# Third instead of fourth: the order of products in seven-product blocks, and three sums that change hands

## The chip, the cores and the metric

The kernel runs on one core of a Trainium2 chip. The metric is device time in microseconds (us) of one execution; a version's time is the median of several executions. The profile is one profiled execution, which traces every instruction with its start, its duration and what it waited for.

## The reference

A two-layer decoder trunk on 256 tokens of width 1024, in float32. Each layer is an FFN, an attention, and a second FFN, each behind an RMS norm and with a residual. The first layer's attention is stick-breaking; the second's is a sliding window with sinks that reads a K/V computed from the stream between the layers. So there are four FFNs, in the order FFN 1, attention, FFN 2, FFN 3, attention, FFN 4:

```python
D_MODEL, SEQ, DEPTH, D_FF = 1024, 256, 2, 2816

def swiglu(x, w_in, w_out):
    gate, up = jnp.split(x @ w_in, 2, axis=-1)
    return (jax.nn.silu(gate) * up) @ w_out

for layer in range(DEPTH):
    h = h + 0.5 * swiglu(rms_norm(h, ffn1_norm[layer]), ffn1_w_in[layer], ffn1_w_out[layer])
    ...                                   # attention, h = h + o @ w_o
    h = h + 0.5 * swiglu(rms_norm(h, ffn2_norm[layer]), ffn2_w_in[layer], ffn2_w_out[layer])
return rms_norm(h, final_norm)
```

## The kernel before

**A product.** A float32 product is made from three matmuls of the type fp32r: each operand is split in a high and a low half, and high x high, low x high and high x low are added up. ScalarE makes the high half of a weight tile (a cast, `w_hi`, L418), VectorE the low half by subtraction (`w_lo`, L420), in two pieces of 128x1024 for each megabyte of weights. A product (`product`, L619) takes a 512x512 piece of weights from its split (L405) through four steps of three matmuls, twelve 512-column matmuls, into one PSUM bank. All matmuls are issued at L287.

**The FFN.** The 2816 columns of an FFN are worked off in blocks: FFN 1 has a plain block, a narrow one of 256 columns and four seven-product blocks of 512 columns; FFNs 2 to 4 have one narrow block (block 0) and five seven-product blocks (blocks 1 to 5). Nineteen seven-product blocks in all, made by `strassen` (L773). The input is cut in 2 x 2 quarters: token half 0 or 1, and upper or lower half of the 1024 features. The weights of a block are cut in 2 x 2 as well: r11 and r21 are the gate's columns on the upper and lower features, r12 and r22 those of the up branch. r21 is thus the lower left piece. Instead of eight quarter products, seven are made, with S0 to S3, sums of the input's quarters that are made once in each FFN (`operand_sums`), and with sums of the weights. Before the change they stand in this order; a, d and b are the block's three PSUM banks:

| | weights | input | into bank | weights' sum made ahead |
|---|---|---|---|---|
| P1 | r11 | token half 0, upper | a | - |
| P2 | r11 | S0 | d | r11 += r12 (sum 0) |
| P3 | r22 | S3 | d, added | - |
| P4 | r21 | token half 0, lower | b | - (the plain product on the lower left weights) |
| P5 | r11 | S1 | a, added | r11 += r22 (sum 1) |
| P6 | r12 | S2 | a, added | r12 += r22 (sum 2) |
| P7 | r11 | token half 1, lower | a, added | r11 += r21 (sum 3) |

Between them stand copies by ScalarE that must be done before the next product adds into the same bank: bank a into b after P1 (L797, in most blocks), bank d into the tile `p5` after P2 (the profile's `p`, L781), bank a into `u2` after P5 (the profile's `u`, L781). VectorE adds banks to them (L785) and multiplies (L788); TensorE turns the result round (`turn`, L676).

**Sums.** A sum is made in one of two ways. `add` (L605) lets VectorE add two pieces of 128x1024 (L610); the right side is then the loaded tile. `fetch` (L614) issues from GpSimd's queue a transfer that reads the megabyte of weights from HBM once more and adds it to the tile in SBUF as it lands (L615), after whoever used the tile's old value has done so. Before the change every seven-product block makes sums 0 and 1 by VectorE and sums 2 and 3 by an adding transfer: 38 such transfers in the FFNs, and three more in the first attention. GpSimd's queue holds, beside these, the small powers of the norms (L522).

**Buffers.** Weights are loaded over SP's queue (`load`, L379) into six tiles of a megabyte, which are handed out in the order in which they were put back: a block takes four, the output weights of the block before take two in turn.

**The output product.** The FFN's second matmul (`out`, L866, `out_step`, L862) on the result of block n - 1 is listed in block n between P6 and P7: eight steps behind the narrow block 0, sixteen behind a seven-product block, a step being three matmuls.

**The order on the engines.** No queue's order is written by hand. The code lists tasks with engine, estimated duration and dependencies (`Plan`); a list scheduler (`listed`, `order`, L195) then simulates all queues. TensorE takes the listed order but, where the next step isn't ready in the simulation, the next one that is; all others take the task with the earliest due time, and the due times come from TensorE's order in the pass before, in up to four passes. The result is a fixed sequence of instructions for each engine with semaphores between. On the chip each engine works its sequence off strictly in order.

Of the kernel before, what the change touches and what calls it, by code (L numbers as in the profile page):

```python
# [18 lines left out]
D = 1024  # L19
# [20 lines left out]
PIECES = 2  # L40
ADDING = 170.0
PLAIN = 330.0
BY_DMA = False
DMA3 = True
FSUMS = 5000.0
TM = 1000.0
BOOST = 10000.0
# [11 lines left out]
LATE = (True, True, True)  # L59
KVFIRST = True  # L60
KVLATE = 3000.0
C11_0 = False
BL_LATE = 0.0

# [149 lines left out]
def dve(n):  # L214
    return n / 0.96 + 70
# [11 lines left out]
def kernel(  # L227
# [34 lines left out]
    RAW, WP, A4 = Slots("raw", RAWS, 8), Slots("w", HL, 8), Slots("a", 4, 4)  # L262
# [17 lines left out]
    def ts(t):  # L280
        return slice(t * P, (t + 1) * P)
# [7 lines left out]
    def B(*bs):  # L289
        return [(b, 0) for b in bs]  # L290
# [109 lines left out]
    def flat(buf):  # L400
        return buf.ap.rearrange("p a b -> p (a b)")
# [3 lines left out]
    def split(raw, prio=None):  # L405
        prio = plan.pos - LEAD if prio is None else prio
        a, b = raw.ab
        if raw.cut == 4:
            return split_fine(raw, prio)
        hi, lo = WP.get([P, a, b], F32R, "w_hi"), WP.get([P, a, b], F32R, "w_lo")  # L410
        m = a * b // PIECES
        for j in range(PIECES):
            sl = slice(j * m, (j + 1) * m)
            ks = [j] if PIECES == 2 else [0, 1]
            rs = [2 * j, 2 * j + 1] if raw.cut == 4 else ks

            first = [(xh, (0, 0))] if raw.cut == 4 and j == 1 else []
            T("ACT", act(m), lambda sl=sl: ACT.copy(out=flat(hi)[:, sl], in_=flat(raw)[:, sl]),  # L418
              r=[(raw, i) for i in rs] + first, w=[(hi, i) for i in ks], prio=prio)
            T("DVE", dve(m), lambda sl=sl: DVE.tensor_sub(out=flat(lo)[:, sl], in0=flat(raw)[:, sl],  # L420
                                                          in1=flat(hi)[:, sl].bitcast(F32)),
              r=[(raw, i) for i in rs] + [(hi, i) for i in ks], w=[(lo, i) for i in ks], prio=prio)
        return hi, lo
# [22 lines left out]
    def by_k(w):  # L446
        return w.rearrange("(k p) n -> p k n", p=P)
# [23 lines left out]
    def of_x(t, k):  # L471
        return ((lambda: xh.ap[:, k, ts(t)], lambda: xl.ap[:, k, ts(t)]), [(xh, (t, k // 4)), (xl, (t, k // 4))])
# [129 lines left out]
    def of_sums(SH, SL, i):  # L602
        return lambda kk: ((lambda: SH.ap[:, i, kk], lambda: SL.ap[:, i, kk]), [(SH, i), (SL, i)])

    def add(dst, src):  # L605
        m = 2048 // PIECES
        for i in range(PIECES):
            sl = slice(m * i, m * i + m)
            ks = [i] if PIECES == 2 else [0, 1]
            T("DVE", dve(m), lambda sl=sl: DVE.tensor_add(out=flat(dst)[:, sl], in0=flat(dst)[:, sl], in1=flat(src)[:, sl]),  # L610
              r=[(src, k) for k in ks], w=[(dst, k) for k in ks], prio=plan.pos - LEAD)


    def fetch(dst, src):  # L614
        T("POOL", 1500, lambda: nc.gpsimd.dma_start(out=dst.ap, in_=src, accum_op=ALU.add), w=[(dst, 0), (dst, 1)],  # L615
          prio=plan.pos - LOADS, lat=500.0)
        T("SP", P * 2048 * 4 / ADDING, lambda: None, w=[(dst, 0), (dst, 1)], prio=plan.pos - LOADS)

    def product(bank, raw, xs, first, last, at=0.0):  # L619
        w = split(raw)  # L620
        for kk in range(4):
            step(bank, w, kk, xs(kk), first and kk == 0, last and kk == 3)
        WP.put(*w)

    def ffn(w_in, w_out, acc, rest, finish, kv=None, blocks=BLOCKS, roots=None, ending=False, there=False, arranged=False):

        first, late = arranged, roots is not None
        wi, wo = by_k(w_in), by_k(w_out)  # L630
        wi4 = w_in.rearrange("(j p k) n -> p j k n", j=2, k=4)
        ring = [banks[i] for i in rest[0:3]]
# [16 lines left out]
        def of_s(i):  # L649
            return of_sums(SH, SL, i)  # L650

        def col(h, i, c, n=512):
            cs = slice(h * DFF + c, h * DFF + c + n)
            return wi4[:, i, :, cs] if first else wi[:, 4 * i:4 * i + 4, cs]

        def silu(dst, src, r, w, t, n=512):
            if late:
                T("ACT", act(n, True), lambda: ACT.activation(out=dst(), in_=src(), func=AF.Silu, scale=roots[t][0].ap), r=r + B(roots[t][0]) + [(consts, "tbl")], w=w)
            else:
                T("ACT", act(n), lambda: ACT.activation(out=dst(), in_=src(), func=AF.Silu), r=r + [(consts, "tbl")], w=w)  # L660
# [9 lines left out]
        def turn(m, t, aT, nk=4):  # L670
            n = nk * P
            view = lambda b: (lambda: b.ap[:, 0:nk, ts(t)])

            def run():
                for i in range(nk):
                    PE.transpose(out=tr.ap[:, i * P:(i + 1) * P], in_=m.ap[:, i * P:(i + 1) * P], identity=ident)  # L676
            T("PE", 109 * nk, run, r=B(m) + ID, w=B(tr))
            STG.put(m)
            part_to(tr, (aT[0], t, view(aT[0])), (aT[1], t, view(aT[1])), n,
                    lambda: tr.ap[:, 0:n].rearrange("p (a b) -> p a b", a=nk))  # L680
# [92 lines left out]
        def strassen(n, c, between):  # L773
            a, d, b = ring
            ring[:] = [d, b, a]
            aT = new_a()
            r11, r12, r22, r21 = [load([(slice(0, 512), col(h, i, c))], 4, 512) for h, i in ((0, 0), (1, 0), (1, 1), (0, 1))]

            def stage(src, name):
                s = STG.get([P, 512], F32, name)  # L780
                T("ACT", act(512), lambda: ACT.copy(out=s.ap, in_=src.ap), r=B(src), w=B(s), prio=plan.pos - STAGE)  # L781
                return s

            def plus(s, bank):
                T("DVE", dve(512), lambda: DVE.tensor_add(out=s.ap, in0=s.ap, in1=bank.ap), r=B(bank), w=B(s))  # L785

            def mul_less(dst, a_, b_, r, w, t):
                T("DVE", dve(512), lambda: DVE.scalar_tensor_tensor(out=dst(), in0=b_(), scalar=roots[t][1].ap if late else -1.0, in1=a_(),  # L788
                                                                    op0=ALU.mult, op1=ALU.mult),
                  r=r + (B(roots[t][1]) if late else []), w=w, lat=LAT["DVE"] + TM)  # L790

            product(a, r11, lambda kk: of_x(0, kk), True, False)
            c11 = C11 and (n != 1 or blocks[0] == "p" or C11_0)
            if c11:
                T("ACT", act(512), lambda: ACT.copy(out=b.ap, in_=a.ap), r=B(a), w=B(b), prio=plan.pos - STAGE)  # L797
                s1 = STG.get([P, 512], F32, "s1")
            else:
                s1 = stage(a, "s1")  # L800
            add(r11, r12)
            product(d, r11, of_s(0), True, False)
            p5 = stage(d, "p5")
            if BY_DMA:
                fetch(r11, col(1, 1, c))
            else:
                add(r11, r22)
            if DMA3:
                fetch(r12, col(1, 1, c))
            else:  # L810
                add(r12, r22)
            product(d, r22, of_s(3), False, True)
            RAW.put(r22)
            product(b, r21, lambda kk: of_x(0, 4 + kk), not c11, True)
            RAW.put(r21)
            if c11:
                silu(lambda: s1.ap, lambda: b.ap, B(b), B(s1), 0)
            else:
                plus(s1, b)
                silu(lambda: s1.ap, lambda: s1.ap, [], B(s1), 0)  # L820
            product(a, r11, of_s(1), False, False)
            fetch(r11, col(0, 1, c))
            u2 = stage(a, "u2")
            plus(u2, d)
            mul_less(lambda: s1.ap, lambda: s1.ap, lambda: u2.ap, B(u2), B(s1), 0)
            STG.put(u2)
            turn(s1, 0, aT)
            product(a, r12, of_s(2), False, False)
            RAW.put(r12)
            plus(p5, a)  # L830
            between()
            product(a, r11, lambda kk: of_x(1, 4 + kk), False, True)
            RAW.put(r11)
            m = STG.get([P, 512], F32, "m")
            silu(lambda: m.ap, lambda: a.ap, B(a), B(m), 1)
            mul_less(lambda: m.ap, lambda: m.ap, lambda: p5.ap, B(p5), B(m), 1)
            STG.put(p5)
            turn(m, 1, aT)
            return aT, 4
# [300 lines left out]
    def shared_kv(vec, other):  # L1140
# [25 lines left out]
        def run(ring, tr):  # L1166
# [19 lines left out]
            at_ = plan.pos  # L1186
            plan.pos += KVLATE
            for t in range(NT):
# [404 lines left out]
```

## Time and profile before

| | |
|---|---|
| median of 3 executions | 911.58 us (910.59 to 912.58) |
| profiled execution: its own time | 910.39 us |
| profiled execution: its span, first to last instruction | 908.6 us |
| mean granted TensorE clock | 0.998 |
| seven-product blocks of FFN 2, FFN 3, FFN 4, about | 307 to 455, 492 to 640, 739 to 892 us |

PE is TensorE, DVE is VectorE, ACT is ScalarE, POOL is GpSimd, SP the queue that issues plain loads. In a row of the timeline the columns are start, duration, engine, line, operation, output <- inputs and shapes; in brackets stands the engine's idle time ahead of it and what ended it. Matmuls overlap and their ends are modelled: a 512-column matmul is shown as 0.39 us long, but the next one starts about 0.23 us after it. Pauses shorter than the overlap are seen in the distance between starts only. In a row of windows each engine has its busy time and, in brackets, its instructions. Names of tiles stand without their numbers: `w_lo,S_h` is a matmul of the low half of weights with the high half of an input sum, `xT` the plain input, `aT` the operand of the output product.

### The profile page before, as it was taken

How to read it: one execution, taken by the hardware profiler on the slowest of the kernel's cores; microseconds unless marked ns; L12 is line 12 of the kernel's file. 1: busy time of each engine (PE TensorE's matmuls, PEld its weight loads, DVE VectorE, ACT ScalarE, POOL GpSimd, SP SyncE). 2: the span in 40 equal slices, each digit the busy share in tenths (PEclk: the TensorE clock that was granted, in tenths of full speed). 3: DMA queues.
4: the chain of work that ended last, by engine and by line, in shares of the span. 5: the costliest groups of instructions: out<-in, count | busy, mean ns of one | idle time of the engine just before them, and what ended most of it. 6: DMA issues, size and time to landing. Idle time of an engine off the chain costs nothing.

```text
span 908.6 us, 11840 instructions
## 1 busy us (share of the span) xinstructions
PE 897.5 (99%) x4420; PEld 739.5 (81%) x4420; DVE 818.3 (90%) x989; ACT 650.1 (72%) x935; POOL 66.7 (7%) x71
## 2 busy tenths in 40 slices
PE   9999999999999999999999999999999999999997
PEld 6888888888888888888888878888897787788886
DVE  8989989687977999998889999999788799999985
ACT  7867667786986876776688767667857677677662
POOL 2001000000000101010000101010000001101000
PEclk9999999999999999999999999999999999999999
DMA  9997999995763499999795999998944149999951
GB/s 337 349 238 223 289 298 233 285 291 154 239 206 115 104 267 306 246 290 268 211 343 127 255 264 266 284 318 225 335 129 163 47 107 287 284 250 291 323 148 47
DMA packets 107305, 214.43 MB, mean 236 GB/s; under 512 B 6256, under 2 KB 27760, under 8 KB 107248
## 3 DMA queue, kind: packets, MB, share of 16 engines
q1 hardware_dynamic: 85184, 170.49, 52.6%
q0 software_dynamic: 21648, 42.99, 26.9%
q8 instruction: 34, 0.56, 0.2%
q10 hardware_dynamic: 416, 0.20, 0.1%
q14 instruction: 23, 0.19, 0.1%
HBM read 212.62 MB, written 1.05 MB: 235 GB/s over the span
## 4 chain that ended last, share of the span: by engine, by line
PE 89%; DVE 8%; ACT 2%; issue 1%; DMA 0%; DVEq 0%; ACTq 0%
PE ps L287 85%; DVE w_lo L420 4%; PE ps L676 2%; ACT w_hi L418 1%; PE ps L490 1%; DVE raw L610 1%; DVE e L1319 0%; PE ps L1327 0%; DMA hN<-in_x_dram 0%; DVE s L586 0%; DVE small L1293 0%; DVE S_l L580 0%; ACT u L781 0%; DVE aT_l L497 0%; DVE o_l L1359 0%
## 5 line engine op out<-in xcount | busy, mean ns | idle before, releaser
L420 DVE TENSOR_TENSOR w_lo<-raw,w_hi 128x1024 fp32r<-128x1024 f32 x424 | 499.8, 1219 | 24.7 <-ACT w_hi L418 23.1
L418 ACT CAST w_hi<-raw 128x1024 fp32r<-128x1024 f32 x424 | 423.0, 1049 | 102.9 <-DVE raw L610 40.0
L287 PE MATMUL ps<-w_hi,xT 128*128 128x512 f32 (+1 forms) x788 | 229.8, 375 | 0.0
L287 PEld LDWEIGHTS ps<-w_hi,xT 128*128 128x128 f32 x788 | 142.7, 188 | 26.6 <-DVE xT L497 0.5
L287 PE MATMUL ps<-w_lo,xT 128*128 128x512 f32 (+1 forms) x394 | 146.8, 373 | 0.0
L287 PE MATMUL ps<-w_hi,aT_h 128*128 128x512 f32 x354 | 139.9, 395 | 0.0
L287 PE MATMUL ps<-w_lo,aT_h 128*128 128x512 f32 x354 | 137.7, 389 | 0.0
L287 PE MATMUL ps<-w_hi,aT_l 128*128 128x512 f32 x354 | 137.5, 388 | 0.0
L287 PE MATMUL ps<-w_hi,S_h 128*128 128x512 f32 x320 | 127.3, 398 | 2.0 <-ACT u L781 1.2
L287 PE MATMUL ps<-w_lo,S_h 128*128 128x512 f32 x320 | 124.9, 390 | 0.0
L287 PE MATMUL ps<-w_hi,S_l 128*128 128x512 f32 x320 | 124.8, 390 | 0.0
L610 DVE TENSOR_TENSOR raw<-raw 128x1024 f32<-128x1024 f32 x78 | 94.6, 1220 | 0.5
L615 POOL DMA_DIRECT2D raw<-in_ffn_w_in_dram x38 | 48.3, 1271 | 507.2 <-DVE w_lo L420 255.3
L287 PEld LDWEIGHTS ps<-w_lo,xT 128*128 128x128 f32 x394 | 74.2, 188 | 13.6 <-DVE w_lo L420 0.4
L287 PEld LDWEIGHTS ps<-w_lo,aT_h 128*128 128x128 f32 x354 | 66.4, 188 | 13.9
L287 PEld LDWEIGHTS ps<-w_hi,aT_l 128*128 128x128 f32 x354 | 66.6, 188 | 13.0
L287 PEld LDWEIGHTS ps<-w_hi,aT_h 128*128 128x128 f32 x354 | 66.5, 188 | 12.8
L287 PEld LDWEIGHTS ps<-w_hi,S_h 128*128 128x128 f32 x320 | 60.1, 188 | 16.8 <-ACT u L781 3.2
L287 PEld LDWEIGHTS ps<-w_lo,S_h 128*128 128x128 f32 x320 | 60.1, 188 | 13.0 <-DVE w_lo L420 0.2
L287 PEld LDWEIGHTS ps<-w_hi,S_l 128*128 128x128 f32 x320 | 60.2, 188 | 11.5
L496 ACT CAST aT_h<-ps 128x512 fp32r<-128x512 f32 (+1 forms) x48 | 26.3, 549 | 49.4 <-PE ps L676 49.2
L287 PE MATMUL ps<-xT,w_hi 128*128 128x512 f32 (+1 forms) x136 | 47.0, 394 | 0.0
(184 smaller groups left out, 941.7 us busy)
## 6 DMA issues: line engine op xcount, KB each, us to landing
raw<-in_ffn_w_in_dram SPq DMA_DIRECT2D x76, 1024.0 KB, 7.5
raw<-in_ffn_w_out_dram SPq DMA_DIRECT2D x44, 1024.0 KB, 8.2
raw<-in_ffn_w_in_dram POOLq DMA_DIRECT2D x38, 1024.0 KB, 10.0
raw<-in_sb_w_qkv_dram SPq DMA_DIRECT2D x12, 1024.0 KB, 8.0
raw<-in_ffn_w_in_dram SPq DMA_DIRECT2D x16, 512.0 KB, 6.4
raw<-in_ffn_w_in_dram SPq DMA_DIRECT2D x16, 256.0 KB, 5.4
raw<-in_sb_w_o_dram SPq DMA_DIRECT2D x4, 1024.0 KB, 5.3
raw<-in_swa_w_q_dram SPq DMA_DIRECT2D x4, 1024.0 KB, 9.0
```

The source lines that it names most:

```text
L287: PE.matmul(ps, lhsT=lhsT, rhs=rhs, start=start, stop=stop, skip_group_check=True)
L418: T("ACT", act(m), lambda sl=sl: ACT.copy(out=flat(hi)[:, sl], in_=flat(raw)[:, sl]), r=[(raw, i) for i in rs] + first, w=[(hi, i) for i i ...
L420: T("DVE", dve(m), lambda sl=sl: DVE.tensor_sub(out=flat(lo)[:, sl], in0=flat(raw)[:, sl], in1=flat(hi)[:, sl].bitcast(F32)), r=[(raw, i) ...
L490: PE.matmul(bank.ap[:, i * P:(i + 1) * P], lhsT=s, rhs=ident, start=i == 0, stop=True, is_transpose=True, skip_group_check=True)
L496: T("ACT", act(n), lambda: ACT.copy(out=hi[2](), in_=src()), r=B(bank), w=[hi[0:2]])
L610: T("DVE", dve(m), lambda sl=sl: DVE.tensor_add(out=flat(dst)[:, sl], in0=flat(dst)[:, sl], in1=flat(src)[:, sl]), r=[(src, k) for k in ks ...
L615: T("POOL", 1500, lambda: nc.gpsimd.dma_start(out=dst.ap, in_=src, accum_op=ALU.add), w=[(dst, 0), (dst, 1)], prio=plan.pos - LOADS, lat=5 ...
L676: PE.transpose(out=tr.ap[:, i * P:(i + 1) * P], in_=m.ap[:, i * P:(i + 1) * P], identity=ident)
```

## The change

A table `SPECIAL` now tells for each seven-product block, by the number of the FFN and of the block, who makes the four sums (V for VectorE, D for an adding transfer), in which order P3 and P4 are listed ((2, 3): P4 first), and behind which product the output product of the block before is listed (4 is the old place, and all have it).

In 18 of the 19 blocks P4 is listed ahead of P3; the 14 of FFNs 1 to 3 (four, five and five; the entry for FFN 1's narrow block is unused) keep their sums as they were. In FFN 4, block 1 keeps the old order of P3 and P4 and makes three sums by adding transfers (sum 1 too); blocks 3 and 4 make sum 3 by VectorE instead of a transfer; blocks 2 and 5 keep theirs. Adding transfers in the FFNs: 38 + 1 - 2 = 37. Additions by VectorE at L610: 78 - 2 + 4 = 80 pieces. r21's tile is put back after its split, which now is ahead of r22's, or, where VectorE makes sum 3, after that sum. `fill` and `stage_` only carry the place and the count.

```diff
--- before.py
+++ after.py
@@ -40,8 +40,6 @@
 PIECES = 2
 ADDING = 170.0
 PLAIN = 330.0
-BY_DMA = False
-DMA3 = True
 FSUMS = 5000.0
 TM = 1000.0
 BOOST = 10000.0
@@ -59,6 +57,7 @@
 LATE = (True, True, True)
 KVFIRST = True
 KVLATE = 3000.0
+SPECIAL = {(1, 1): ('VVDD', (2, 3), 4), ... (4, 1): ('VDDD', (3, 2), 4), (4, 2): ('VVDD', (2, 3), 4), (4, 3): ('VVDV', (2, 3), 4), (4, 4): ('VVDV', (2, 3), 4), (4, 5): ('VVDD', (2, 3), 4)}
 C11_0 = False
 BL_LATE = 0.0
 
@@ -624,9 +623,12 @@
 
 
 
+    stage_ = []
+
     def ffn(w_in, w_out, acc, rest, finish, kv=None, blocks=BLOCKS, roots=None, ending=False, there=False, arranged=False):
 
         first, late = arranged, roots is not None
+        stage_.append(0)
         wi, wo = by_k(w_in), by_k(w_out)
         wi4 = w_in.rearrange("(j p k) n -> p j k n", j=2, k=4)
         ring = [banks[i] for i in rest[0:3]]
@@ -798,37 +800,52 @@
                 s1 = STG.get([P, 512], F32, "s1")
             else:
                 s1 = stage(a, "s1")
-            add(r11, r12)
+            makers, second, filled = SPECIAL.get((len(stage_), n), ("VVDD", (3, 2), 4))
+
+            def fill(q):
+                if q == filled:
+                    between()
+
+
+            def summed(i, dst, src, h, k):
+                if makers[i] == "D":
+                    fetch(dst, col(h, k, c))
+                else:
+                    add(dst, src)
+
+            summed(0, r11, r12, 1, 0)
             product(d, r11, of_s(0), True, False)
             p5 = stage(d, "p5")
-            if BY_DMA:
-                fetch(r11, col(1, 1, c))
-            else:
-                add(r11, r22)
-            if DMA3:
-                fetch(r12, col(1, 1, c))
-            else:
-                add(r12, r22)
-            product(d, r22, of_s(3), False, True)
-            RAW.put(r22)
-            product(b, r21, lambda kk: of_x(0, 4 + kk), not c11, True)
-            RAW.put(r21)
+            summed(1, r11, r22, 1, 1)
+            summed(2, r12, r22, 1, 1)
+            for q in second:
+                if q == 3:
+                    product(d, r22, of_s(3), False, True)
+                    RAW.put(r22)
+                else:
+                    product(b, r21, lambda kk: of_x(0, 4 + kk), not c11, True)
+                    if makers[3] == "D":
+                        RAW.put(r21)
             if c11:
                 silu(lambda: s1.ap, lambda: b.ap, B(b), B(s1), 0)
             else:
                 plus(s1, b)
                 silu(lambda: s1.ap, lambda: s1.ap, [], B(s1), 0)
+            fill(6)
             product(a, r11, of_s(1), False, False)
-            fetch(r11, col(0, 1, c))
+            summed(3, r11, r21, 0, 1)
+            if makers[3] != "D":
+                RAW.put(r21)
             u2 = stage(a, "u2")
             plus(u2, d)
             mul_less(lambda: s1.ap, lambda: s1.ap, lambda: u2.ap, B(u2), B(s1), 0)
             STG.put(u2)
             turn(s1, 0, aT)
+            fill(7)
             product(a, r12, of_s(2), False, False)
             RAW.put(r12)
             plus(p5, a)
-            between()
+            fill(4)
             product(a, r11, lambda kk: of_x(1, 4 + kk), False, True)
             RAW.put(r11)
             m = STG.get([P, 512], F32, "m")
```

More of the change, by code (lines that the diff above doesn't have):

```diff
@@ L61 @@
 KVLATE = 3000.0
+SPECIAL = {(1, 1): ('VVDD', (2, 3), 4), (1, 2): ('VVDD', (2, 3), 4), (1, 3): ('VVDD', (2, 3), 4), (1, 4): ('VVDD', (2, 3), 4), (1, 5): ('VVDD', (2, 3), 4), (2, 1): ('VVDD', (2, 3), 4), (2, 2): ('VVDD', (2, 3), 4), (2, 3): ('VVDD', (2, 3), 4), (2, 4): ('VVDD', (2, 3), 4), (2, 5): ('VVDD', (2, 3), 4), (3, 1): ('VVDD', (2, 3), 4), (3, 2): ('VVDD', (2, 3), 4), (3, 3): ('VVDD', (2, 3), 4), (3, 4): ('VVDD', (2, 3), 4), (3, 5): ('VVDD', (2, 3), 4), (4, 1): ('VDDD', (3, 2), 4), (4, 2): ('VVDD', (2, 3), 4), (4, 3): ('VVDV', (2, 3), 4), (4, 4): ('VVDV', (2, 3), 4), (4, 5): ('VVDD', (2, 3), 4)}
 C11_0 = False
```

## The prediction

> **What bounds the kernel now.** I read the page first: shares, chain, groups, queues.
>
> ```profile
> span 908.6 us, 11840 instructions
> ...
> PE 897.5 (99%) x4420; PEld 739.5 (81%) x4420; DVE 818.3 (90%) x989; ACT 650.1 (72%) x935; POOL 66.7 (7%) x71
> ...
> q1 hardware_dynamic: 85184, 170.49, 52.6%
> q0 software_dynamic: 21648, 42.99, 26.9%
> ...
> PE 89%; DVE 8%; ACT 2%; issue 1%; DMA 0%; DVEq 0%; ACTq 0%
> ...
> L610 DVE TENSOR_TENSOR raw<-raw 128x1024 f32<-128x1024 f32 x78 | 94.6, 1220 | 0.5
> L615 POOL DMA_DIRECT2D raw<-in_ffn_w_in_dram x38 | 48.3, 1271 | 507.2 <-DVE w_lo L420 255.3
> ...
> raw<-in_ffn_w_in_dram POOLq DMA_DIRECT2D x38, 1024.0 KB, 10.0
> ```
>
> TensorE bounds it: 89% of the chain, and neither order nor sums change how many matmuls there are. So the change can only win or lose pauses of TensorE. Next come the windows, one for the blocks of each of the FFNs 2 and 3, and the last FFN cut in three.
>
> ```profile
> core 0: us, PE busy (x) PEld busy (x) DVE busy (x) ACT busy (x) POOL busy (x), PEclk, DMA share, GB/s
> 307.00:455.00 148.00, 148.00 (x671) 121.98 (x670) 142.05 (x144) 103.73 (x125) 11.53 (x9) 1.00 0.88 254
> 492.00:640.00 148.00, 147.44 (x666) 120.87 (x665) 143.06 (x143) 104.80 (x126) 11.49 (x9) 1.00 0.91 259
> 739.00:816.00 77.00, 75.53 (x337) 60.87 (x337) 76.59 (x80) 55.40 (x68) 6.39 (x5) 1.00 0.91 253
> 816.00:860.00 44.00, 44.00 (x202) 36.36 (x201) 41.90 (x41) 29.04 (x33) 3.84 (x3) 1.00 0.99 311
> 860.00:892.00 32.00, 32.00 (x148) 26.52 (x147) 27.50 (x28) 20.03 (x25) 1.28 (x1) 1.00 0.53 126
> ```
>
> The first half of the last FFN stands out: VectorE works 76.59 of 77.00 us there and TensorE has gaps of 1.47; afterwards TensorE has none and VectorE has 2.1 + 4.5 us to spare. VectorE makes the low halves of the weights, so in that half TensorE lives from hand to mouth. "PE busy" hides small pauses, because matmuls overlap; the spacing of their starts shows them. The chain gives the undisturbed pace:
>
> ```profile
> 786.35 15.70 PE ps L287 x69
> ```
>
> 15.70 / 69 = 0.2275 us. In the timeline of TensorE these are the largest pauses among the blocks that the change touches (last FFN, blocks 2, 2 and 3; FFN 3, blocks 4 and 2):
>
> ```profile
> 769.91 0.39 PE L287 MATMUL ps<-w_lo,S_h 128*128 128x512 f32 x1
> 770.97 0.50 PE L287 MATMUL ps<-w_hi,S_h 128*128 128x512 f32 x1 [0.68 <-ACT p L781]
> 771.31 0.39 PE L287 MATMUL ps<-w_hi,S_l 128*128 128x512 f32 x1
> ...
> 781.15 0.39 PE L287 MATMUL ps<-w_lo,S_h 128*128 128x512 f32 x1
> 782.21 0.50 PE L287 MATMUL ps<-w_hi,S_h 128*128 128x512 f32 x1 [0.68 <-ACT u L781]
> 782.55 0.39 PE L287 MATMUL ps<-w_hi,S_l 128*128 128x512 f32 x1
> ...
> 813.00 0.39 PE L287 MATMUL ps<-w_lo,aT_h 128*128 128x512 f32 x1
> 813.51 0.50 PE L287 MATMUL ps<-w_hi,S_h 128*128 128x512 f32 x1
> 813.84 0.39 PE L287 MATMUL ps<-w_hi,S_l 128*128 128x512 f32 x1
> ...
> 587.83 0.39 PE L287 MATMUL ps<-w_lo,xT 128*128 128x512 f32 x1
> 588.24 0.50 PE L287 MATMUL ps<-w_hi,S_h 128*128 128x512 f32 x1
> 588.58 0.40 PE L287 MATMUL ps<-w_hi,S_l 128*128 128x512 f32 x1
> ...
> 533.41 0.39 PE L287 MATMUL ps<-w_lo,aT_h 128*128 128x512 f32 x1
> 534.33 0.50 PE L287 MATMUL ps<-w_hi,S_h 128*128 128x512 f32 x1 [0.54 <-ACT u L781]
> 534.67 0.40 PE L287 MATMUL ps<-w_hi,S_l 128*128 128x512 f32 x1
> ```
>
> Each costs its wait and a slow second start. 769.91 to 771.31 is 1.40 for two steps of 0.2275: 0.94 us lost. Likewise 781.15 to 782.55: 0.94; 813.00 to 813.84: 0.84 - 0.455 = 0.39; 587.83 to 588.58: 0.75 - 0.455 = 0.29; 533.41 to 534.67: 0.81. Together 3.37 us, nearly all that there is to win. The last one waits for the copy u, which the change does not move, in an FFN whose sums stay as they are: I leave it.
>
> **The change, part by part.** *The order.* P4 now stands between P2 and P3. It adds no instruction. At 770.97 TensorE had ended P2 and could not start P3, which adds into the same bank, until ScalarE had copied that bank (p). P4 writes another bank and fits in. In most blocks it already does in part: the planner draws two of P4's four steps forward (at 588.24 they stand ahead of the wait), and there a full P4 instead of half changes nothing but the 0.29 at 588. P4's own bank must be free:
>
> ```profile
> 768.97 0.69 ACT L658 ACTIVATE m<-ps,small 128x512 f32<-128x512 f32 x1 [2.14 <-PE ps L287]
> 769.70 0.57 ACT L797 COPY ps<-ps 128x512 f32<-128x512 f32 x1
> 770.33 0.59 ACT L781 COPY p<-ps 128x512 f32<-128x512 f32 x1
> ```
>
> The copy into it ends at 770.27, P2 at 769.91 + 0.23 = 770.14: P4 starts about 0.2 late. Credit 0.94 - 0.2 = 0.74 here, and 0.29 at 588. In turn r21's split is due 2.72 us (12 x 0.2275) earlier and r22's 2.72 later; these are the same VectorE pieces in another order, and r21's buffer instead of r22's comes free first for the next block's r11: priced at nothing, because the next block's loads wait for whichever comes first. On SP's queue the loads of r21 and r22 may swap, which moves either by one transfer, 2.9 us of the DMA engines (52.6% of 908.6 / 163 transfers, the 170.49 MB of q1); half of P4 stood in third place before, so r21 was wanted there already. Past 816 VectorE's 6.6 us of idle time cover it; where they are gone, a swapped split costs one piece, 1.2 us.
>
> *Block 1 of the last FFN.* The sum r11 + r22 leaves VectorE (two pieces):
>
> ```profile
> 737.49 1.22 DVE L420 TENSOR_TENSOR w_lo<-raw,w_hi 128x1024 fp32r<-128x1024 f32 x1
> ...
> 744.56 1.22 DVE L610 TENSOR_TENSOR raw<-raw 128x1024 f32<-128x1024 f32 x1
> 745.70 1.22 DVE L420 TENSOR_TENSOR w_lo<-raw,w_hi 128x1024 fp32r<-128x1024 f32 x1
> ```
>
> Starts lie 1.14 apart (744.56 to 745.70), so VectorE is 2.28 us earlier from block 1's second half on. TensorE's pauses are what VectorE needed to keep up, so relief here is what lets pauses go: 0.94 at 782 (P6 waits for the copy u, and any ready step of the FFN's output product would fill it), and about half of the 0.39 at 813, say 0.2 (there the copy also queued behind a cast). The relief is spent by that: 0.74 + 0.94 + 0.2 = 1.88 of 2.28.
>
> In exchange comes a second adding transfer, of r22 into r11, between P2's split and P5's.
>
> ```profile
> 735.37 1.32 POOL L615 DMA_DIRECT2D raw<-in_ffn_w_in_dram  x1 [1.68 <-DVE raw L610]
> ...
> 744.08 1.05 ACT L418 CAST w_hi<-raw 128x1024 fp32r<-128x1024 f32 x1 [0.90 <-DMA raw<-in_ffn_w_in_dram]
> ...
> 750.40 0.39 PE L287 MATMUL ps<-w_hi,S_h 128*128 128x512 f32 x1
> ```
>
> The first one takes 735.37 to 744.08, 8.7 us. P2's split ends by 738.63, so the second is issued at about 739.0. Two at once are not in the trace. Low bound: they overlap freely, 739.0 + 8.7 = 747.7. High bound: it starts when the first has landed and then takes the page's median of 10.0, 754.1. Nearest row: a transfer's pure time, 26.9% of 908.6 us / 41 transfers (42.99 MB) = 5.96 us, behind the first: 744.1 + 6.0 = 750.1; I take that. A cast (1.05) and a subtraction (1.22) later, at 752.4, P5 can run; it stood at 750.40. Eight steps of block 0's output product (24 x 0.2275 = 5.46 us) can stand ahead of it: 2.0 us take three, and the pause for u takes two more. Cost 0; where it lands after 752.2, too few are left for u and 0.84 us appears; after 753.6 each microsecond costs one. At 754.1 that is 0.84 + 0.5 = 1.3. P5's cast waits on ScalarE's queue for this landing: behind it stand p, u and the silu, so a late landing delays those too. POOL holds nothing else behind it but the block's third transfer.
>
> [...]
>
> *Blocks 3 and 4.* r11 + r21 goes back to VectorE: 2 x 2.28 = 4.56 us. Cover: block 1's relief less what the pauses spent (0.4), and the idle 2.1 us up to 860 and 4.5 after. Bounds: nothing, or one sum uncovered, 2.28. P7's weights no longer wait for a landing; by that the early work on the next block's r11 can step back, so I take 0.1. If the cover is gone, P7 of block 3 (826) is what comes late. Two adding transfers (2 x 5.96 us of the DMA engines) leave a stretch where their share is 0.99, one joins where it is 0.91: no credit, as TensorE does not wait for them there.
>
> **Sum.** -0.74 - 0.94 - 0.2 - 0.29 + 0.1 = -2.07 us, or 908.3 against the profiled execution's 910.39. The median of the runs is 1.19 above that execution: 911.58 - 2.07 = 909.5. About 0.2% (1.8 us) is what a measurement of this kernel tells from no change: 909.8 and 913.4 are the marks.
>
> **Rivals.** *Half of it.* The order closes 0.74 and 0.29, but the pause at 782 stays or returns a product later, since VectorE has under 0.4 us over. For it: 76.59 of 77.00. Against: 2.28 us are more than the pauses need. About 911.58 - 1.0 = 910.6.
>
> *Nothing moves.* The planner already fills the gaps, the pauses come back elsewhere: 911.6. For it: in FFN 2, with the order alone changed, TensorE has 148.00 of 148.00.
>
> *Slower.* The second transfer of block 1. It decides when it lands after 753.6. To be 1.8 us slower while the order still saves 1.0, it must cost 2.8: 0.84 + 2.0, a landing at 755.6, beyond the high bound, with the plain loads of the next block sharing its engines: 5.9 us (two plain loads of 2.9) added to 750.1 gives 756.0, cost 0.84 + 2.4, less the 1.0 saved: 913.8. Against: 744.08 shows that the first, beside little else, is quick.
>
> [...]
>
> *More.* Also the rest at 813 (0.19), the 0.81 at 534, should r21's earlier splits free a filler there, and the 0.2 of P4's late start; about a half more elsewhere: 907.8.
>
> **Chances.** Forecast 0.45 (own range 908.7 to 909.8), more 0.05, half 0.30, nothing 0.10, slower 0.08, the rule 0.02. Faster 0.45 + 0.05 = 0.50; same 0.40; slower 0.10. Range 908.1 to 912.0: it takes in forecast, half and nothing, 0.85.
>
> **What would show it.** Right: no wait for p at L781 in the last FFN's block 2 and none for u; L610 x80, POOL's L615 x37; two POOL issues within some 4 us near 735 to 740, and ScalarE released by the second landing near 750; VectorE over 41.9 us between 816 and 860 with TensorE still without gaps. Wrong: a new gap of TensorE ahead of P5 at 750 or P7 near 826, or the 0.94 at 782 standing in another place; pauses outside the FFNs that shift, since the planner orders the whole program anew.

## The result, and the profile after

The changed kernel took 909.5 us (median of 20 runs, 908.24 to 913.19), the kernel before 910.95 us (20 runs, 909.92 to 912.58). The ratio is 0.9985 with the interval 0.9979 to 0.9991: 1.45 us faster by the medians, where 2.07 had been forecast. The profiled execution took 910.13 us.

The page of the changed kernel, rows that answer to those of before:

```profile
span 908.3 us, 11837 instructions
...
PE 896.8 (99%) x4420; PEld 741.2 (82%) x4420; DVE 819.8 (90%) x991; ACT 649.7 (72%) x935; POOL 65.9 (7%) x70
...
PE 83%; DVE 7%; DMA 4%; issue 3%; ACT 1%; POOL 0%; POOLq 0%; DVEq 0%; ACTq 0%
...
L609 DVE TENSOR_TENSOR raw<-raw 128x1024 f32<-128x1024 f32 x80 | 97.0, 1223 | 0.5
...
L614 POOL DMA_DIRECT2D raw<-in_ffn_w_in_dram x37 | 47.0, 1271 | 508.7 <-DVE raw L609 212.6
```

The matmuls are the same 4420. One adding transfer fewer and two VectorE pieces more are there as announced. The third row is the chain, the work that ended last, followed back step by step to what released it: TensorE's share of it fell from 89% to 83%, and DMA came up from 0% to 4%. The chain now runs through transfers. The windows of the changed kernel, the last FFN's two that matter:

```profile
739.00:816.00 77.00, 75.84 (x343) 62.17 (x342) 76.76 (x81) 57.62 (x72) 5.60 (x5) 1.00 0.96 260
816.00:860.00 44.00, 44.00 (x202) 36.44 (x201) 43.90 (x43) 27.53 (x32) 1.56 (x2) 1.00 0.83 274
```

In the first half TensorE got six matmuls more into 77 us (x343 against x337): 6 x 0.2275 = 1.4 us. In the second stretch VectorE is full (43.90 of 44.00), and TensorE still has no gap.

A sharper view than windows at fixed times is the time between the same two matmuls of both programs, counted by number. From the matmul at 705.9 to the one at 821.8 us (before) the distance fell from 115.95 to 114.76, so 1.19 us of the gain lie in the first half of the last FFN. From 472 to 574 us, with FFN 3's first blocks, it rose from 102.08 to 102.35 (ahead of 472 the two programs order the end of FFN 2 differently, and the same number is not the same matmul), from 574 to 689 us it fell from 114.94 to 114.61, and from 821.8 to 902 us it went from 80.33 to 80.30. FFN 3 as a whole thus gained next to nothing.

The span of the profiled execution is only 0.3 us shorter (908.6 to 908.3), because 1.04 us were lost ahead of the first place where TensorE's order differs: the matmul at 41.34 us before, which has the same place in that order in every version, stands at 42.38 here. That is scatter between executions. Over the 14 traces it stands at 41.11 to 42.46 us, latest in the kernel with the sums alone, whose TensorE order is that of before up to the last FFN.

Behind these small sums old pauses went and new ones came. This is what TensorE waited for between 305 and 905 us, first the kernel before, then the changed one (columns: us in total, times, longest):

```profile
PE ps L287 <- ACT u L781: 1.2, 2, 0.7
...
PE ps L287 <- ACT p L781: 0.7, 1, 0.7
```

```profile
PE ps L286 <- ACT u L783: 1.2, 1, 1.2
PE ps L286 <- ACT p L783: 1.2, 1, 1.2
```

Two waits for u became one, the wait for p stayed, and each is now longer. They are at new places. TensorE's timeline of the changed kernel:

```profile
564.92 0.39 PE L286 MATMUL ps<-w_lo,aT_h 128*128 128x512 f32 x1
566.50 0.50 PE L286 MATMUL ps<-w_hi,S_h 128*128 128x512 f32 x1 [1.19 <-ACT u L783]
566.83 0.39 PE L286 MATMUL ps<-w_hi,S_l 128*128 128x512 f32 x1
...
769.48 0.50 PE L286 MATMUL ps<-w_hi,S_h 128*128 128x512 f32 x1 [1.16 <-ACT p L783]
769.82 0.39 PE L286 MATMUL ps<-w_hi,S_l 128*128 128x512 f32 x1
```

564.92 to 566.83 is 1.91 for two steps, 1.46 us lost (FFN 3, block 3, where nothing stood before). The pause at 769.48 (last FFN, block 2) costs 1.43 by the same count, in place of the 0.94 at 771. Gone are 0.94 at 782, 0.81 at 534, 0.29 at 588, a pause of 0.27 at 515, and 0.17 of the 0.39 at 813. Most of what is missing to the 1.19 us are stretched starts of 0.04 to 0.15 us each at 766, 772 and 778, which are gone as well.

What makes these two late is in the chain. Two windows of it, 540 to 570 and 740 to 772 us, of the changed kernel:

```profile
547.88 12.16 DMA raw<-in_ffn_w_in_dram
...
560.07 2.96 ACT w_hi L417 x3
...
565.87 0.59 ACT u L783
...
566.50 3.71 PE ps L286 x15
```

```profile
738.18 11.25 DMA raw<-in_ffn_w_in_dram
...
755.64 11.28 DMA raw<-in_ffn_w_in_dram
...
766.95 2.00 ACT w_hi L417 x2
768.94 0.49 ACT p L783
...
769.48 2.56 PE ps L286 x10
```

ScalarE's timeline shows what came later still, the copy from bank a to bank b that P4 of block 2 needs (769.70 before):

```profile
773.94 0.57 ACT L799 COPY ps<-ps 128x512 f32<-128x512 f32 x1
```

Both windows of the chain read alike: an adding transfer lands late, the cast that waits for it blocks ScalarE's queue, and the copy behind that cast is what TensorE waits for. Before, the first of these ran thus (ScalarE's timeline): no cast waited, and u came at 564.19 instead of 565.87.

```profile
556.55 5.80 ACT L418 CAST w_hi<-raw 128x1024 fp32r<-128x1024 f32 x6
...
564.19 0.59 ACT L781 COPY u<-ps 128x512 f32<-128x512 f32 x1 [0.32 <-PE ps L287]
```

**Theories.** At 566, *the freed buffer*: with P4 third, r21's buffer comes free first and the next block's r11 load takes it. Before, it took r22's buffer, which VectorE still had to read for sum 1, so the load left later. SyncE's issues of before, then of after:

```profile
557.36 8.25 SPq L368 DMA_DIRECT2D raw<-in_ffn_w_in_dram  x4
```

```profile
552.68 13.42 SPq L367 DMA_DIRECT2D raw<-in_ffn_w_in_dram  x4
```

The load now leaves at 552.68, while the adding transfer (issued 547.88) is still under way, and they share the 16 engines: 12.16 us to land instead of 10.36. From 552.68 to the landing at 560.04, 7.36 us, the queue of the adding transfers moved 0.94 MB and that of the plain loads 1.01 MB; before, in the last 5.56 us ahead of the landing, the first moved 0.84 MB and the second none. A part of the delay is older than the load: in the first 4.80 us from its issue the transfer had moved 0.11 MB, before 0.20. So the load does not wait behind the transfer; that it slows it is the theory, and the runs below agree (9.8 to 10.6 us without the early load, 11.0 to 13.8 with it). Rivals: the copies are late by ScalarE's or VectorE's own queue, or landings scatter by chance. At 769, *the second transfer of block 1* delays P5, P5 delays the issue of sum 3's transfer (755.64; before 751.87), and that delays P7 and p. Rival: block 1's sums would be as late in any form. GpSimd's issue of sum 3's transfer before:

```profile
751.87 1.27 POOL L615 DMA_DIRECT2D raw<-in_ffn_w_in_dram  x1 [15.17 <-DVE w_lo L420]
```

### The profile page after: what moved, and what is told of

The parts are those of the page before. It is cut to its first block, busy times and chain, and to the rows that moved or that the text cites. A ratio compares the mean times of both kernels' runs of the same rounds, so it can differ in the third digit from the quotient of the medians.

```text
span 908.3 us, 11837 instructions
## 1 busy us (share of the span) xinstructions
PE 896.8 (99%) x4420; PEld 741.2 (82%) x4420; DVE 819.8 (90%) x991; ACT 649.7 (72%) x935; POOL 65.9 (7%) x70
## 4 chain that ended last, share of the span: by engine, by line
PE 83%; DVE 7%; DMA 4%; issue 3%; ACT 1%; POOL 0%; POOLq 0%; DVEq 0%; ACTq 0%
PE ps L286 79%; DMA raw<-in_ffn_w_in_dram 4%; DVE w_lo L419 3%; PE ps L678 2%; PE ps L489 1%; ACT w_hi L417 1%; DVE raw L609 1%; DVE e L1336 0%; PE ps L1344 0%; DVE s L585 0%; DVE S_l L579 0%; DVE small L1310 0%; DVE o_l L1376 0%; DVE aT_l L496 0%; PE ps L1269 0%
## 5 line engine op out<-in xcount | busy, mean ns | idle before, releaser
L609 DVE TENSOR_TENSOR raw<-raw 128x1024 f32<-128x1024 f32 x80 | 97.0, 1223 | 0.5
L614 POOL DMA_DIRECT2D raw<-in_ffn_w_in_dram x37 | 47.0, 1271 | 508.7 <-DVE raw L609 212.6
```

## The experiments

Where an edit is a table entry, the letters say who makes sums 0 to 3 (V VectorE, D an adding transfer), and (2, 3) that P4 goes ahead of P3, (3, 2) the old order. The key is (FFN, block). The kernel before, run beside them, had medians of 911.14, 911.72 and 911.46 us in the three groups of runs; ratios are to it.

**1. The two halves of the change, each alone.** The order alone:

```diff
-(4, 1): ('VDDD', (3, 2), 4), ... (4, 3): ('VVDV', (2, 3), 4), (4, 4): ('VVDV', (2, 3), 4)
+(4, 1): ('VVDD', (3, 2), 4), ... (4, 3): ('VVDD', (2, 3), 4), (4, 4): ('VVDD', (2, 3), 4)
```

> P4 ahead of P3 in the same 18 blocks, all sums made as before the change. Theory (the order moves pauses in FFN 3 and does not close those of FFN 4): FFN 3 loses the pauses at 515, 534 and 588 (1.4 us) and gets the new one of 1.46 near 566, FFN 4 keeps pauses of about 2.4 us in its first 75 us; about 0.0 to 0.5 us faster than before. Rival (the prediction's step): the order closes 0.74 in FFN 4 and 0.29 in FFN 3, about 1.0 us faster.

The sums alone (every (2, 3) of the table back to (3, 2)):

```diff
-(1, 1): ('VVDD', (2, 3), 4), ... (4, 5): ('VVDD', (2, 3), 4)
+(1, 1): ('VVDD', (3, 2), 4), ... (4, 5): ('VVDD', (3, 2), 4)
```

> The old order of P3 and P4 everywhere; in FFN 4 block 1 makes three sums by adding transfers, blocks 3 and 4 make sum 3 by VectorE. Theory: the relief of VectorE is what FFN 4 gained, so 1.2 us faster than before (the first 77 us of FFN 4's blocks by 1.2 shorter, FFN 3 as before with its pauses at 515, 534, 588). Rival: sums and order are needed together; then under 0.5 us faster.

The order alone: 910.5 us, ratio 0.9993 [0.9984, 1.0002], not told from no change. The sums alone: 909.39 us, 0.9978 [0.9970, 0.9987], all that the whole change brings. TensorE's waits under the order alone, 305 to 905 us:

```profile
PE ps L286 <- ACT w_hi L417: 1.0, 1, 1.0
PE ps L286 <- DVE w_lo L419: 1.0, 2, 0.5
PE ps L286 <- ACT u L783: 0.9, 2, 0.7
```

FFN 3's pauses at 534 and 588 are gone, as after. The one at 534 goes with the order: it stands (0.79 to 0.87 us) in all five traces with the old order in that block and in none of the nine with the new one. The one at 588 is no such case: of the five traces with the old order there it is missing in two (the sums alone, and blocks 3 and 4 alone), and in another it is 0.60 us.

In the last FFN, where block 1 is as before the change in this run, P4 does what was forecast of it. TensorE's timeline:

```profile
771.66 0.50 PE L286 MATMUL ps<-w_hi,xT 128*128 128x512 f32 x1
...
778.99 0.50 PE L286 MATMUL ps<-w_lo,S_h 128*128 128x512 f32 x1 [0.45 <-DVE w_lo L419]
...
783.59 0.50 PE L286 MATMUL ps<-w_hi,S_h 128*128 128x512 f32 x1 [0.68 <-ACT u L783]
```

P4 (`xT`) runs where P3 had waited for p, and by the count of two steps the 0.94 at 771 is down to 0.32. But a new pause of 0.72 stands at 779, for VectorE's `w_lo`, and the 0.94 for u is still there. So of the forecast 0.74 only 0.4 are left in that FFN (212.85 us from 689 to 902, before 213.23). A further new pause stands at 448, 1.2 us and 0.69 behind it, ahead of FFN 2's last P7. That is no steady result of the order: the program up to the last FFN is the same as the changed kernel's, where the same transfer landed in 12.0 us instead of 14.81 and nothing waited.

**2. Which sums.** Only block 1 of the last FFN changed, in the old order; then only blocks 3 and 4:

```diff
-(4, 1): ('VVDD', (3, 2), 4)
+(4, 1): ('VDDD', (3, 2), 4)
```

> The kernel before, except that block 1 of FFN 4 makes sum 1 by a transfer too; blocks 3 and 4 keep their transfers, the order is the old one. Theory (the relief of VectorE in block 1 is the whole gain): 1.2 to 1.7 us faster than before, the stretch from 689 on 1.2 shorter. Rival (blocks 3 and 4 matter, since two transfers less leave the loads of blocks 4 and 5 earlier, or since VectorE's relief is spent without them): under 0.7 us faster, or pauses past 816.

```diff
-(4, 3): ('VVDD', (3, 2), 4), (4, 4): ('VVDD', (3, 2), 4)
+(4, 3): ('VVDV', (3, 2), 4), (4, 4): ('VVDV', (3, 2), 4)
```

> The kernel before with one part of the change alone: in blocks 3 and 4 of the last FFN sum 3 (r11 + r21) is made by VectorE instead of an adding transfer; old order, block 1 as before. Theory: VectorE's idle time past 816 covers the two sums, TensorE does not wait for them: no pause of TensorE past 816 and the time of the kernel before within 0.3 us, ratio 0.9997 to 1.0003 of it (the median of the other kernel's runs here is the mark). Rival (the sums are not covered): a pause ahead of P7 of block 3 near 826 or of block 4 near 843, up to 2.28 us each, 912 to 914. Rival (two adding transfers fewer relieve the loads): 0.5 to 1 us faster, about 910.5.

Block 1 alone: 910.58 us, 0.9985 [0.9971, 0.9999]. Its last FFN is as short as the changed kernel's (211.85 us between the matmuls that stand 213.23 apart before and 212.0 after). The wait for p near 769 is there too, with the old order (1.50 us lost; 1.54 with the sums alone): it comes with block 1's second transfer and not with the order. Blocks 3 and 4 alone: 911.68 us, 1.0005 [0.9991, 1.0018], no change. Their window past 816 us:

```profile
816.00:860.00 44.00, 43.91 (x200) 36.05 (x199) 43.97 (x44) 27.99 (x32) 1.27 (x1) 1.00 0.83 277
```

VectorE took the two sums up to 43.97 of 44.00. Without block 1's relief they are not free: a pause of 0.36 us stands at 837, where none was expected, and the distance from 821.8 to 902 us is 80.68 instead of 80.33. With that relief they are (80.30 in the changed kernel). So the gain is block 1's sum; the two later ones win nothing.

**3. The pause at 566.** First the buffer alone: r21's is given back behind r22's, the order of the products stays.

```diff
-                    if makers[3] == "D":
-                        RAW.put(r21)
...
+            if makers[3] == "D":
+                RAW.put(r21)
```

> The changed kernel, except that r21's buffer is put back behind r22's, so that the next block's first load waits for P3's split as it did before the change; the order of the products stays. Theory (the next block's first load, 4.7 us earlier, shares the DMA engines with the adding transfer of sum 2 in block 3 of FFN 3; its landing is 2.3 us later, ScalarE stands in its cast, the copy u behind it is late): that transfer lands within 10 us of its issue, the pause of 1.46 near 566 is gone, time 1 to 1.4 us below the changed kernel. Rival (the order of ScalarE's queue makes the pause, the load has no part in it): the pause stays at over 1.2 us and the time is that of the changed kernel.

918.61 us, 1.0086 [1.0073, 1.0099], a miss. The pause at 566 did shrink to 0.31 us, with its transfer at 10.29 us; but the loads, held longer, now bunch around sum 3's transfer of each FFN's last block (in FFN 3 three loads of weights are issued beside it, two in the changed kernel). The chain near FFN 3's end:

```profile
623.92 15.87 DMA raw<-in_ffn_w_in_dram
...
639.81 1.05 ACT w_hi L417
...
642.17 4.21 PE ps L286 x11
```

These transfers took 15.56, 15.01 and 15.87 us in FFNs 1, 2 and 3, with losses of 3.3, 2.6 and 4.7 us behind them, the last with slow matmuls after the pause (eight from 642.70 to 645.20 us, at a granted clock of 0.60). The buffer's release does set when transfers land; holding it everywhere moves the loss to a worse place. Then only the block that suffers, with the old order:

```diff
-(3, 3): ('VVDD', (2, 3), 4)
+(3, 3): ('VVDD', (3, 2), 4)
```

> The changed kernel with one block of 18 back in the old order: block 3 of FFN 3 (P3 ahead of P4); all sums as in the change. Theory (the freed buffer): r22's buffer is again the one that comes free first for this block's last load, it has VectorE as a second reader, so the next block's r11 load goes out some 4 to 5 us later and sum 2's adding transfer lands within 10.5 us of its issue (12.16, 13.30 and 13.77 us in three executions with the new order here). The pause of TensorE near 566 (1.46 us, 2.6 in another execution) goes, and the time falls by that much, 1.2 to 2.5 us against the changed kernel's 909.5: 907.0 to 908.4. Rival (the buffer only moves the bunching): the pause appears one or two blocks later, or ahead of the last P7 of FFN 3 near 641, and the time is 909 to 912. Rival (chance of the execution): the landings scatter between 9 and 14 us whatever the order; then the transfer here takes over 11 us with the old order too.

908.65 us, 0.9966 [0.9954, 0.9979]. SyncE's issue of the load and ScalarE's copy u are back where they were, and of the waits for ScalarE's copies in TensorE's list only p is left (three views, in this order):

```profile
557.20 8.28 SPq L367 DMA_DIRECT2D raw<-in_ffn_w_in_dram  x4
```

```profile
564.02 0.58 ACT L783 COPY u<-ps 128x512 f32<-128x512 f32 x1
```

```profile
PE ps L286 <- ACT p L783: 1.1, 1, 1.1
```

The transfer landed in 10.59 us, no pause followed later in FFN 3, and the stretch from 472 to 574 us fell to 101.17 us (after 102.35). The profile's span is 906.5. By the medians the gain is 0.9 us, just short of the 1.2 expected, and the ratio's interval overlaps the changed kernel's: the trace shows the pause gone, the times alone would not.

Third, the transfer taken away, with the new order kept:

```diff
-(3, 3): ('VVDD', (2, 3), 4)
+(3, 3): ('VVVD', (2, 3), 4)
```

> The changed kernel, new order everywhere, but in block 3 of FFN 3 sum 2 is made by VectorE (two pieces of 1.22 us, starts 1.14 us apart) instead of an adding transfer. Theory (the transfer's late landing makes the pause near 566): without that transfer no cast waits for it, the copy u is not late, and the pause of 1.46 us is gone; VectorE is 2.28 us later in this block, and since VectorE bounds the stretch 492 to 640 by 2 to 3 us of slack, up to 1.1 us can come back as small pauses before 640: 908.2 to 909.5. Rival (the copy u is late because of ScalarE's or VectorE's own queue, not the transfer): the pause near 566 stays or grows by up to 2.28 us: 909.5 to 911.8.

915.91 us, 1.0045 [1.0029, 1.0061]. Near 566 only 0.29 us is left by the count of two steps, so all beyond that was the transfer's, and neither engine's own queue. The price was far off. With VectorE 2.28 us behind, later transfers came late: the one issued at 591.63 took 15.05 us (8.83 in the changed kernel), and the last was issued at 623.83 instead of 619.57. The chain:

```profile
591.63 15.05 DMA raw<-in_ffn_w_in_dram
...
606.70 1.06 ACT w_hi L417
...
617.01 0.76 DVE m L790
...
617.81 0.66 PE ps L678 x4
```

Pauses of 2.95 us at 617.81 and 3.0 at 638.83 to 640.09 follow. Up to 1.1 us had been allowed for such pauses; the kernel came out 6.4 above the changed one.

Over all executions with this transfer the landing goes with the early load: 12.16, 11.15, 10.98, 13.30 and 13.77 us with it (the order alone and block 1's other form among them); 10.36, 10.05, 10.43, 9.82, 10.29, 10.59, 10.36 and 10.11 without. The two groups do not overlap. Within the first, the pause differs from execution to execution and grows with the landing: 0.32 us (landing 10.98), 0.47, 1.46, 2.60 and 2.98 (landing 13.77). About 0.3 of it is not this transfer's: that much stands with the buffer held (0.31) and with no transfer (0.29).

**4. The pause at 769.** Block 1 with the transfer for sum 0 instead of sum 1:

```diff
-(4, 1): ('VDDD', (3, 2), 4)
+(4, 1): ('DVDD', (3, 2), 4)
```

> The changed kernel, except that in block 1 of FFN 4 sum 0 is made by the adding transfer and sum 1 by VectorE: the same relief of VectorE, but P5 no longer waits for a second transfer, and sum 3's transfer, which waits for P5's split, is issued earlier. Theory (the pause of 1.43 at 769 comes from sum 3's late landing at 766.9, which holds ScalarE's queue ahead of the copy p, and P7, whose bank P4 of block 2 needs): that transfer is issued by about 752 instead of 755.6, the pause at 769 is below 0.3, time about 1 us below the changed kernel unless P2 waits for the first transfer. Rival (the pause at 769 is VectorE's lag that found another place): a pause of over 1 us stays in the first 77 us of FFN 4's blocks.

913.61 us, 1.0030 [1.0018, 1.0042], 4.1 above the changed kernel, where about 1 below it had been expected. Sum 3's transfer left at 749.16 and landed in time (758.53), and the pause at 769 was gone: the chain named above holds. But later transfers landed late:

```profile
858.95 13.84 DMA raw<-in_ffn_w_in_dram
...
877.28 0.49 ACT u L783
...
877.82 2.35 PE ps L286 x9
```

A pause of 2.42 us at 877.82, and 0.37 to 1.3 at 742, 793 and 843.7, cost more than the 1.43. Why these transfers were slow was not tried.

**5. Spread, and a better version.** The changed kernel once more; with sum 3 of each FFN's last block by VectorE; the same sums in the old order.

> The changed kernel once more, beside the others on one chip. Theory (the sums give the gain, the order gives nothing): 1.2 to 1.7 us faster than before, within 0.7 us of the version with the sums alone. Its trace shows whether the pauses near 566 (1.46) and in the last block of FFN 2 (none in the first trace, 1.9 in that of the order alone, which is the same program up to FFN 4) differ from execution to execution: theory, that they do, by over 0.5 us, with the landing of the adding transfer they wait for. Rival (the plan fixes them): the same pauses within 0.2 us.

```diff
-(1, 5): ('VVDD', (2, 3), 4), (2, 5): ..., (3, 5): ..., (4, 5): ('VVDD', (2, 3), 4)
+(1, 5): ('VVDV', (2, 3), 4), (2, 5): ..., (3, 5): ..., (4, 5): ('VVDV', (2, 3), 4)
```

> The changed kernel, and sum 3 of the last block of each FFN by VectorE instead of a transfer, four transfers less. Theory (the last P7 of an FFN waits now and then for that transfer, whose landing moved from 11.5 to 15.9 us after its issue between traces): no pause ahead of P7 in the last blocks, time about 0.3 to 0.8 us below the changed kernel and a narrower spread of its runs. Rival (VectorE, with 2.28 us more in each FFN, is late in its place): the time is that of the changed kernel or above, with pauses of P7 that wait for w_lo.

```diff
-(1, 5): ('VVDD', (2, 3), 4), ... and (2, 3) in all other blocks
+(1, 5): ('VVDV', (3, 2), 4), ... and (3, 2) in all other blocks
```

> The sums of the change with the old order of P3 and P4 everywhere, and sum 3 of each FFN's last block by VectorE. Theory: with the old order the last transfers landed in time in both traces (12.5 to 13.1 us after their issue, no pause), so nothing changes against the sums alone: 1.2 to 1.9 us faster than before. Rival (any transfer less helps): over 2.2 us faster.

The changed kernel again: 909.52 us, 0.9973 [0.9964, 0.9982]; its pause near 566 was 2.49 us this time, 2.60 with a slow second start, while FFN 2's last transfer landed in 11.55 us and nothing waited for it. With VectorE's last sums: 908.46 us, 0.9970 [0.9955, 0.9986], runs from 907.6 to 913.77, not the narrower spread that was expected; the profiled one took 912.7 and lost 4.6 us near 567. The same sums in the old order: 912.4 us, 1.0008 [0.9993, 1.0023], slower than without them (909.39), a miss; its profiled execution was the shortest of its runs and shows, beside what the sums alone have, only 0.99 us at 162, so the cause stays open. Last, block 3 of FFN 3 in the old order and the last sums by VectorE together:

> The changed kernel with two edits together: block 3 of FFN 3 in the old order, and in the last block of each of the four FFNs sum 3 made by VectorE instead of an adding transfer. Each edit aims at one late transfer: sum 2's in block 3 of FFN 3 (12 to 14 us with the new order) and sum 3's of the last blocks (12 to 15 us). If both causes hold and VectorE has room at the FFNs' ends: 1.2 to 2.5 us from the first and about 1 from the second (the second alone measured 908.5 against 909.5): 906.5 to 908. Rival: with the old order in the block, the sums by VectorE at the ends come late, as in the kernel of the old order with these sums (912.4): 909 to 912.

907.51 us (907.43 to 909.16), 0.9956 [0.9939, 0.9973], as expected and the fastest of all; 3.95 us under the kernel before beside it. The interval lies below that of the changed kernel's first comparison, and overlaps that of its second. TensorE's waits between 305 and 905 us:

```profile
PE ps L286 <- ACT p L783: 1.0, 1, 1.0
PE ps L286 <- ACT o_h L1370: 0.5, 1, 0.5
PE ps L286 <- ACT qT L500: 0.5, 1, 0.5
PE ps L1344 <- ACT ws L500: 0.2, 1, 0.2
```

The first edit's part is as in experiment 3 (101.08 us from 472 to 574). The second's is not where it was expected: the last blocks lost little in these executions anyway; 0.75 us went between 689 and 706 us (16.15 us, else 16.9), where the planner laid the work out anew and a wait of 0.7 for o_l is gone. From 821.8 to 902 us 0.5 was lost (80.78, in the changed kernel 80.30). Why the planner came to this is open.

## Why the prediction was right, step by step

- **The median and its sign: right.** 909.5 forecast, 909.5 measured, though part of that is luck: the kernel before ran at 910.95 here, 0.6 below the 911.58 that the sum started from, and the gain was 1.45 and not 2.07. Errors also cancelled: in the profiled execution the order's largest term lost 0.49 us instead of winning 0.74, and two pauses that the sum left out, 534's 0.81 and 515's 0.27, went and paid for most of the new one at 566 (1.46).
- **0.94 at 782, by block 1's relief of VectorE: right.** The pause is gone, also with block 1's sum alone. So is about 0.2 at 813 (0.17 measured).
- **0.74 at 771, by the order: right alone, wrong beside block 1's second transfer.** With the order alone P4 filled the place: 0.94 became 0.32, near the 0.2 that was taken. The pause at 779, for VectorE's low half, then took most of it back. In the changed kernel the step failed. The prediction asked only that P4's bank be free of the a-to-b copy, and took the time of that copy from the kernel before. P4's bank hangs on P7 of the block before, and P7 on sum 3's transfer. That landed at 766.92 instead of 761.22, the copy came at 773.94 instead of 769.70, and P4 ran behind P3. The whole change turned 0.94 into 1.43. Of the signs named for being right, "no wait for p" in block 2 is the one that did not come.
- **Second transfer in block 1, cost 0: its landing right, its price mis-sized.** Landing 749.43 against 750.1 taken. P5 came at 754.08, output-product steps filled up to it, and no pause stood there. But the step ended with P5; what P5 releases (sum 3's transfer) was not followed. That wait is the 1.43 at 769, and it stands in the old order as well.
- **0.29 at 588, by the order: not shown.** It is gone, but it was also gone in two traces with the old order. 534's 0.81, left out because the change was said not to move the copy u, did go by the order.
- **"r21's buffer instead of r22's comes free first, priced at nothing": wrong.** It moves the next load 4.7 us earlier into an adding transfer, and the pause near 566 is then 0.3 to 3 us. In the profiled execution this eats what the order wins in FFN 3: from 472 to 689 us it is 217.03 before, 216.96 after, and 215.91 with that one block in the old order. In the trace of the order alone the pause was only 0.47, and the two at 448 took the gain, so that the order's median shows no gain is not put down to this block alone.
- **Blocks 3 and 4, +0.1: near enough** beside block 1's relief (80.33 to 80.30); alone they cost 0.35.
- **"The rule", 0.02: no run shows it.** The 37 issues of adding transfers in the FFNs average 1271 ns, as the 38 did before; block 1's first two took 1.32 and 1.30 us, and the second transfer landed at 749.43.

## What to carry to other kernels

Moving a product changes when its weight buffer comes free, and so which transfer the next load runs into (here a load left 4.7 us earlier, and the transfer took 12.16 us instead of 10.36); follow that load before the buffer is priced at nothing. For an adding transfer follow what its consumer issues next, and what stands behind its cast on the same engine (here the copy u, 1.68 us later), one block further than seems needed. Where one block of many suffers from an order that helps the others, give that block the old order, and read the gain from its own pause, since the medians of runs blur a microsecond (here 0.9 us, with intervals that overlap).

## What was not expected of the hardware

The time from issue to landing of a 1 MB adding transfer was 8.4 to 13.4 us in the changed kernel's profiled execution and up to 15.87 in that with the buffer held, and for one and the same instruction it differed by up to 3.3 us between executions (FFN 2's last, 14.81 with the order alone and 11.55 in the changed kernel's second trace, with the same TensorE order up to the last FFN).

Behind a pause of 3.0 us TensorE's granted clock was 0.52 for the next 3 us. This was in the kernel without sum 2's transfer, around 640 us; TensorE's timeline and then two windows (the granted clock is the third number from the right):

```profile
638.83 0.73 PE L286 MATMUL ps<-w_hi,xT 128*128 128x512 f32 x2 [2.15 <-ACT w_hi L417]
640.09 0.80 PE L286 MATMUL ps<-w_lo,xT 128*128 128x512 f32 x1 [0.53 <-DVE w_lo L419]
```

```profile
640.30:643.30 3.00, 3.00 (x8) 2.35 (x9) 3.00 (x4) 1.80 (x2) 0.00 (x0) 0.52 0.30 72
643.40:646.40 3.00, 3.00 (x14) 2.45 (x14) 1.39 (x2) 2.25 (x3) 0.00 (x0) 1.00 1.07 368
```

Eight matmuls in 3.0 us at a granted clock of 0.52, then 14 at 1.00. By the count of steps about 1.5 us were lost by it, 1.4 of them in the six steps from 640.09 to 642.82 (2.73 us instead of 6 x 0.2275), beside a pause of 3.0. A lower granted clock also stands behind the 2.6 us near 641 in the kernel with the buffer held (0.60, eight matmuls in 2.5 us), and behind the 2.9 us near 567 in the one with VectorE's last sums (0.65, eleven in 4.0 us); behind the 2.95 us at 617.81 in the execution above (1.00, 20 in 4.0 us), and behind 2.49 in the changed kernel's second trace (1.00, 21 in 4.0 us), it did not happen. Pauses of like length thus had a lower clock behind them in three of these places and not in two; why stays open.
